# A hybrid decoder layer on one core: the last four down pairs take two token ranges behind one another, and a range's norm follows its last pair

## The chip, the cores and the metric

One core of a Trainium2 chip runs one program. TensorE (PE) multiplies into PSUM, VectorE (DVE), ScalarE (ACT) and GpSimd (POOL) work on SBUF, SyncE (SP) and GpSimd issue the DMAs here. The metric is the time of one execution on the device, in microseconds; less is better.

## The reference

One decoder layer on 16 learned meta tokens, 1024 prompt tokens and 8 x 8 sample tokens, in float32: two gated recurrent branches, their merge, then an MLP, each with an RMS norm before and after. The change is in the last part:

```python
    hn = rms_norm(x, gains[2])
    ff = jnp.square(jax.nn.relu(hn @ w_up)) @ w_down
    x = x + rms_norm(ff, gains[3])
```

`hn` is (tokens, 1024), `w_up` 1024 x 4096, `w_down` 4096 x 1024. Only the prompt tokens and the sample tokens (1088) go through the MLP.

## The kernel before, in words

Activations lie with the features on the 128 partitions and the tokens along the free axis. The tokens are cut into two halves of 544 columns, which one Strassen step treats as the two column blocks of a product; so a weight *pair* (2 x 2 blocks of 512 x 128) needs seven products instead of eight. They are taken in the order S3, S1, A11, S2, A22, S4, A12, each for the 544 columns of a half in ranges. Each operand is split into a high and a low float16 part, and a product is 4 k blocks x 3 matmuls (high x high, high x low, low x high): 12 matmuls, 84 for a pair and a range.

The MLP's hidden features are worked in four groups (`g`); each group has four up pairs, which write the squared ReLU and its Strassen sums, split, into `aoh` and `aol` (second index the operand of the product, third the up pair), and four down pairs (`o` = 0 to 3), which add into `facc`. Up to the last up pair (group 3, pair 3) columns go in two windows of 272. The split of an up window's result is finished in three parts (`rest`), during the next window; the last window's parts follow behind the loop. Its lines L1547, L1551 and L1556 (ScalarE, high parts), L1554, L1557 and L1558 (VectorE, low parts) write columns 272 to 543 of k block 3.

The last four down pairs are taken by the loop at the end. `LCH` cuts 544 columns into ranges of 272, 144 and 128. `pairc` does a pair on a range: two copies from PSUM by ScalarE (L1426, L1430), two steps by VectorE (L1428, L1432), and seven adds into `facc` (`dn_fin`, L1469 to L1475). Then the squares of the result are added up in `sacc`, and the result is scaled by the gain (ScalarE). When all four pairs of a range are done, `norm_out` normalizes it: L1659 sums over the partitions on TensorE, L424 takes the power on GpSimd, L429 broadcasts on TensorE, L1669 multiplies, L1670 adds the residual (`xr`), and L1671 stores. `norm_out` is a generator; `bgN.step`, called after each product, advances it by estimated time, so that its matmuls lie between later products.

The weights of a pair are prepared by `prep`: two of its four blocks come by DMA into `ws`, two are summed by accumulating DMAs into `sa`; ScalarE (L190) and VectorE (L191) split each operand into `sh` and `sl`; then further accumulating DMAs (GpSimd, L222, L225, L231, and SP, L228) turn the same buffers into the next operands. Both buffers are double. Pair 0's weights are split in the loop before; those of pairs 1 to 3 are all issued ahead of the last loop, into 21 slots.

TensorE's order is that of the code (`manual_schedule`). In the last loop the order of the other engines is made by a scheduler from estimated times; on the chip each engine then goes through its list.

Of the kernel before, what the change touches and what calls it, by code (L numbers as in the profile page):

```python
# [7 lines left out]
F32 = mybir.dt.float32  # L8
F16 = mybir.dt.float16
U8 = mybir.dt.uint8  # L10
AF = mybir.ActivationFunctionType
OP = mybir.AluOpType
# [3 lines left out]
P = 128  # L16
# [12 lines left out]
CQ = HW // 2  # L29
UW = 3 + NPR + NB * (3 + LS)  # L30
CW = UW - 3
NG = 4
# [6 lines left out]
LCH = [(0, 272), (272, 144), (416, 128)]  # L39
# [28 lines left out]
def layer_kernel(ctx, tc, xT, w_pl, w_pr, w_o, w_up, w_dn, gw, par, sconv, slru, shg,  # L68
                 cident, cmask, crow, yT, o_conv, o_h, o_sp, o_ss):
    nc = tc.nc  # L70
    ACT, DVE, POOL, PE = nc.scalar, nc.vector, nc.gpsimd, nc.tensor

    def sbuf(c, name, bufs=1, side="left", fine=True):
        return c.enter_context(tc.tile_pool(name=name, bufs=bufs, side=side, reuse_waits="tile" if fine else "pool"))
# [13 lines left out]
    def nm(s):  # L88
        cnt[0] += 1
        return f"{s}_{cnt[0]}"  # L90
# [156 lines left out]
    def take(**kw):  # L247
        drain(cur["gen"])
        ops = cur["ops"]
        begin(**kw)  # L250
        return ops
# [31 lines left out]
    def prod(o, op, B, nk, c0, w, first):  # L283
        h, l = op
        bh, bl = B
        for k in range(nk):
            PE.matmul(o, h[:, k, :], bh[:, k, c0:c0 + w], start=first and k == 0, stop=False,  # L287
                      skip_group_check=not first)
            PE.matmul(o, h[:, k, :], bl[:, k, c0:c0 + w], start=False, stop=False, skip_group_check=not first)  # L289
            PE.matmul(o, l[:, k, :], bh[:, k, c0:c0 + w], start=False, stop=(k == nk - 1),  # L290
                      skip_group_check=not first)
# [128 lines left out]
    def rs_pow(ps, n, pool, bias):  # L420
        t = pool.tile([P, n], F32, tag="st", name=nm("st"))
        DVE.tensor_scalar(t, ps[:, :n], bias, None, op0=OP.add)
        rs = pool.tile([P, n], F32, tag="rs", name=nm("rs"))
        POOL.tensor_tensor(rs, t, mhalf[:, :n], op=OP.pow)  # L424
        return rs

    def rs_bcast(rs, items, ps):
        for i, skip, n, off in items:
            PE.matmul(ps[:, off:off + n], rs[:, i:i + 1].to_broadcast([P, P]), ident[:, skip:skip + n],  # L429
                      start=True, stop=True)  # L430

    def chunk_tiles(w):
        starts, items = [], []
        o = 0
        while o < w:
            n = min(P, w - o)
            s = o if n == P else w - P
            items.append((len(starts), P - n, n, o))
            starts.append(s)
            o += n  # L440
        return starts, items
# [138 lines left out]
    g0, hl, hp, hk, nhk, n4sp, p2sp, rbh, ibh, gnp, g1, g2, g3 = (sm[:, i, :] for i in range(13))  # L580
# [332 lines left out]
    with tc.manual_schedule(engines={E.PE, E.DVE, E.Pool, E.Activation}):  # L913
# [28 lines left out]
        for n in range(4):  # L942
            e, c0 = n % 2, n // 2 * CT
# [321 lines left out]
    def qbank():  # L1265
        return pq.tile([P, 512], F32, tag="q", name=nm("q"))

    ep = sbuf(ctx, "ep")
# [44 lines left out]
    bgN = Steps()  # L1313
# [70 lines left out]
    for n, (c0, w) in enumerate(WIN):  # L1384
        bgN.drain(n - 2)
        for half in range(2):
            t0 = half * HW + c0
            xx = n3.tile([P, KT, WM], F32, tag=f"x2{half}", name=nm("x2c"))
            acc = n3.tile([P, 2, WM], F32, tag="acc", name=nm("acc"))
# [25 lines left out]
    def pairc(ops, B, c0, w, fin, hook=None):  # L1415
        b4, b3, b1, b2 = qbank(), qbank(), qbank(), qbank()
        U = uvp.tile([P, 2, CT], F32, tag="U", name=nm("U"))
        u, v = U[:, 0, :w], U[:, 1, :w]

        def p(b, name, bi, first):  # L1420
            prod(b[:, :w], ops[name], B(bi), 4, c0, w, first)
            if hook:
                hook(12 * (w / 2400 + 0.0025))

        p(b3, "S3", 5, True)
        ACT.activation(v, b3[:, :w], AF.Copy)  # L1426
        p(b4, "S1", 3, True)
        DVE.tensor_tensor(v, v, b4[:, :w], op=OP.add)  # L1428
        p(b1, "A11", 0, True)
        ACT.activation(u, b1[:, :w], AF.Copy)  # L1430
        p(b2, "S2", 4, True)
        DVE.tensor_tensor(u, b2[:, :w], u, op=OP.subtract)  # L1432
        p(b3, "A22", 6, False)
        p(b4, "S4", 2, False)
        p(b1, "A12", 1, False)
        fin(b1[:, :w], b3[:, :w], b4[:, :w], u, v, c0, w)
# [23 lines left out]
    def dn_fin(g, o):  # L1460
        def fin(b1, b3, b4, u, v, c0, w):
            f11, f21, f12, f22 = (mlp["facc"][:, q // 2, 2 * o + q % 2, c0:c0 + w] for q in range(4))
            if g == 0:
                DVE.tensor_tensor(f22, u, v, op=OP.subtract)
                DVE.tensor_tensor(f21, u, b3, op=OP.subtract)
                DVE.tensor_tensor(f12, b4, u, op=OP.subtract)
                ACT.activation(f11, b1, AF.Copy)
            else:
                DVE.tensor_tensor(f22, f22, u, op=OP.add)  # L1469
                DVE.tensor_tensor(f21, f21, u, op=OP.add)  # L1470
                DVE.tensor_tensor(f12, f12, u, op=OP.subtract)
                DVE.tensor_tensor(f22, f22, v, op=OP.subtract)
                DVE.tensor_tensor(f21, f21, b3, op=OP.subtract)
                DVE.tensor_tensor(f12, f12, b4, op=OP.add)
                DVE.tensor_tensor(f11, f11, b1, op=OP.add)  # L1475
        return fin
# [24 lines left out]
    facc = fp.tile([P, 2, KT, HW], F32, name="facc")  # L1501
# [128 lines left out]
    l2 = sbuf(ctx, "l2", 2)  # L1630
    lslot = (single(l1) for _ in range(21))
    lops = [take(slot=lslot)]
# [7 lines left out]
    def norm_out(c0, w, sacc):  # L1640
        starts, items = chunk_tiles(w)
        ns = len(starts)
        n = 4 if w <= 144 else 2
        todo = [(half, j) for half in (1, 0) for j in range(0, KT, n)]
        xrs = {}

        def load(i):
            if i < len(todo):
                half, j = todo[i]
                t = l2.tile([P, 576], F32, tag="xr", bufs=4, name=nm("xr"))[:, :n * w].rearrange("p (j t) -> p j t", j=n)  # L1650
                nc.sync.dma_start(t, x2_d[:, j:j + n, half * HW + c0:half * HW + c0 + w])
                xrs[i] = t

        for i in range(4):
            load(i)
        ps = qbank()
        for half in (1, 0):
            for i, s in enumerate(starts):
                PE.matmul(ps[:, half * ns + i:half * ns + i + 1], sacc[:, half, 0, s:s + P], ones, start=True, stop=True)  # L1659
        rs = rs_pow(ps, 2 * ns, l2, D * EPS * KD * KD)  # L1660
        yield 4.5
        pss = {}
        for half in (1, 0):
            pss[half] = qbank()
            rs_bcast(rs[:, half * ns:(half + 1) * ns], items, pss[half])
        for i, (half, j) in enumerate(todo):
            t0 = half * HW + c0
            f = facc[:, half, j:j + n, c0:c0 + w]
            DVE.tensor_tensor(f, f, pss[half][:, None, :w].to_broadcast([P, n, w]), op=OP.mult)  # L1669
            (POOL if i % 2 == 0 else DVE).tensor_tensor(f, f, xrs[i], op=OP.add)  # L1670
            nc.sync.dma_start(yT[:, j:j + n, t0:t0 + w], f)  # L1671
            load(i + 4)
            yield 1.5

    for c0, w in LCH:
        sacc = l2.tile([P, 2, 2, CQ], F32, tag="sacc", bufs=1, name=nm("sacc"))
        for o in range(4):
            pairc(lops[o], BA, c0, w, dn_fin(NG - 1, o), bgN.step)
            for half in (1, 0):
                src = facc[:, half, 2 * o:2 * o + 2, c0:c0 + w]  # L1680
                acc = sacc[:, half, :, :w]
                if o == 0:
                    ACT.activation(acc, src, AF.Square)
                else:
                    s = l2.tile([P, 2, CQ], F32, tag="s", name=nm("s"))
                    ACT.activation(s[:, :, :w], src, AF.Square)
                    (POOL if c0 == 0 and o < 3 else DVE).tensor_tensor(acc, acc, s[:, :, :w], op=OP.add)
                    if o == 3:
                        DVE.tensor_tensor(acc[:, 0], acc[:, 0], acc[:, 1], op=OP.add)
                for r in range(2):  # L1690
                    ACT.activation(src[:, r], src[:, r], AF.Copy, scale=g3[:, 2 * o + r:2 * o + r + 1])
        bgN.drain()
        bgN.add(norm_out(c0, w, sacc), 3.0)
    bgN.drain()


# [83 lines left out]
```

## Time and profile before

| | us |
|---|---|
| median of 3 runs | 1927.18 |
| lowest, highest | 1926.94, 1930.95 |
| the profiled execution | 1927.69 |
| its span, first to last instruction | 1925.9 |
| first matmul of the last four down pairs | about 1813.8 |

Times in rows are microseconds from the start of the span. In a row of instructions the second number is how long the group lasted; consecutive instructions of an engine overlap a little, so the step from one to the next is shorter than the duration of one. In brackets stands the idle time of the engine ahead of the row, and what ended it.

### The profile page before, as it was taken

What the parts mean: (1) busy time and instruction counts of PE and PEld (TensorE: products, weight loads), DVE (VectorE), ACT (ScalarE), POOL (GpSimd) and SP (SyncE); (2) the same over time, 40 slices, a digit from 0 to 9 for tenths busy, and PEclk for the clock granted to TensorE, in tenths of its full rate; (3) what the DMA queues carried; (4) which work ended last, traced back from release to release, by engine and by line L of the source; (5) the groups of instructions that cost most, each with busy time, mean ns of one, the idle gap of its engine ahead of it and who ended that gap; (6) DMA issues with size and microseconds to landing.
All of it is one profiled execution on the core that took longest, in us unless ns stands there. A gap on an engine that the chain in (4) does not pass through costs nothing. (4 is left out here: it accounts for less than half of the span.)

```text
span 1925.9 us, 43547 instructions
## 1 busy us (share of the span) xinstructions
PE 1780.8 (92%) x17856; PEld 1519.6 (79%) x17856; DVE 1472.3 (76%) x2654; ACT 1013.9 (53%) x2126; POOL 558.4 (29%) x626
## 2 busy tenths in 40 slices
PE   5999999999999988886899899889999999999897
PEld 4888898898888766665677689878888888888676
DVE  7998989788865888877886867697557757756767
ACT  4555555555445767754443445467346436526653
POOL 3522111211222233436442335562111111111122
PEclk9899999999999998998999999899999999999998
DMA  5252332433346433446778744234545554544635
GB/s 179 61 115 75 85 103 69 123 76 86 94 130 159 103 90 86 106 136 191 224 213 243 235 108 115 59 75 105 116 105 106 114 110 94 115 107 104 133 72 164
DMA packets 117335, 230.30 MB, mean 120 GB/s; under 512 B 11152, under 2 KB 45328, under 8 KB 114064
## 3 DMA queue, kind: packets, MB, share of 16 engines
q0 software_dynamic: 45184, 97.28, 25.6%
q1 hardware_dynamic: 62704, 125.24, 19.9%
q10 hardware_dynamic: 9248, 5.02, 1.0%
q8 instruction: 139, 2.28, 0.5%
q14 instruction: 60, 0.49, 0.1%
HBM read 191.43 MB, written 36.06 MB: 118 GB/s over the span
## 5 line engine op out<-in xcount | busy, mean ns | idle before, releaser
L289 PEld LDWEIGHTS <-sh 128*128 128x128 f16 x3920 | 387.3, 99 | 157.5 <-issue 87.1
L287 PEld LDWEIGHTS <-sh 128*128 128x128 f16 x3920 | 388.3, 99 | 82.9 <-ACT sh L190 7.0
L290 PEld LDWEIGHTS <-sl 128*128 128x128 f16 x3920 | 387.8, 99 | 80.4 <-DVE sl L191 7.6
L287 PE MATMUL pd<-tsh,sh 128*128 128x276 f16 (+1 forms) x960 | 272.4, 284 | 22.3 <-ACT th L405 8.5
L289 PE MATMUL pd<-tsl,sh 128*128 128x276 f16 (+1 forms) x960 | 272.4, 284 | 0.0
L290 PE MATMUL pd<-tsh,sl 128*128 128x276 f16 (+1 forms) x960 | 272.0, 284 | 0.0
L287 PE MATMUL q<-aoh,sh 128*128 128x272 f16 (+2 forms) x1008 | 260.5, 268 | 7.5 <-ACT sh L190 6.1
L290 PE MATMUL q<-aoh,sl 128*128 128x272 f16 (+2 forms) x1008 | 260.6, 268 | 3.6 <-DVE sl L191 3.6
L287 PE MATMUL q<-hoh,sh 128*128 128x272 f16 (+2 forms) x952 | 255.5, 273 | 6.1 <-DVE U L1518 3.6
L289 PE MATMUL q<-aol,sh 128*128 128x272 f16 (+2 forms) x1008 | 260.6, 268 | 0.0
L191 DVE SCALAR_TENSOR_TENSOR sl<-ws,sh 128x512 f16<-128x512 f32 x288 | 210.2, 733 | 63.3 <-ACT sh L190 62.6
L290 PE MATMUL q<-hoh,sl 128*128 128x272 f16 (+2 forms) x952 | 255.5, 273 | 1.0 <-DVE sl L191 1.0
L289 PE MATMUL q<-hol,sh 128*128 128x272 f16 (+2 forms) x952 | 255.5, 273 | 0.6 <-DVE hol L1288 0.6
L287 PE MATMUL pd<-xh,sh 128*128 128x276 f16 (+1 forms) x776 | 222.3, 287 | 36.2 <-ACT U L308 19.5
L191 DVE SCALAR_TENSOR_TENSOR sl<-sa,sh 128x512 f16<-128x512 f32 x201 | 151.1, 754 | 133.0 <-ACT sh L190 131.8
L289 PE MATMUL pd<-xl,sh 128*128 128x276 f16 (+1 forms) x776 | 222.7, 287 | 0.0
L190 ACT ACTIVATE sh<-ws 128x512 f16<-128x512 f32 x288 | 173.8, 622 | 92.5 <-PE pd L289 63.3
L290 PE MATMUL pd<-xh,sl 128*128 128x276 f16 (+1 forms) x776 | 222.5, 287 | 0.0
L190 ACT ACTIVATE sh<-sa 128x512 f16<-128x512 f32 x201 | 124.7, 623 | 124.3 <-DMA sa<-in_w_pr 57.1
L852 PE MATMUL pd<-sh,xh 128*128 128x128 f16 (+1 forms) x576 | 103.4, 222 | 2.3 <-ACT F L366 2.0
L854 PE MATMUL pd<-sh,xl 128*128 128x128 f16 (+1 forms) x576 | 103.5, 222 | 0.0
L853 PE MATMUL pd<-sl,xh 128*128 128x128 f16 (+1 forms) x576 | 103.4, 222 | 0.0
(360 smaller groups left out, 4243.6 us busy)
## 6 DMA issues: line engine op xcount, KB each, us to landing
sa<-in_w_pr POOLq DMA_DIRECT2D x105, 256.0 KB, 4.7
ws<-in_w_pr SPq DMA_DIRECT2D x35, 512.0 KB, 3.5
sa<-in_w_up POOLq DMA_DIRECT2D x48, 256.0 KB, 3.7
sa<-in_w_dn POOLq DMA_DIRECT2D x48, 256.0 KB, 3.8
sa<-in_w_pr SPq DMA_DIRECT2D x35, 256.0 KB, 3.3
ws<-in_w_pr POOLq DMA_DIRECT2D x35, 256.0 KB, 5.9
ws<-in_w_pr SPq DMA_DIRECT2D x35, 256.0 KB, 4.8
th<-th POOLq DMA_DIRECT2D x16, 544.0 KB, 7.1
```

The source lines that it names most:

```text
L190: ACT.activation(hi, src, AF.Copy, scale=SW)
L191: DVE.scalar_tensor_tensor(lo, src, SW, hi, op0=OP.mult, op1=OP.subtract)
L287: PE.matmul(o, h[:, k, :], bh[:, k, c0:c0 + w], start=first and k == 0, stop=False, skip_group_check=not first)
L289: PE.matmul(o, h[:, k, :], bl[:, k, c0:c0 + w], start=False, stop=False, skip_group_check=not first)
L290: PE.matmul(o, l[:, k, :], bh[:, k, c0:c0 + w], start=False, stop=(k == nk - 1), skip_group_check=not first)
L852: PE.matmul(po, a, wh[:, k % 4, :], start=(k == 0), stop=False)
L853: PE.matmul(po, a, wl[:, k % 4, :], start=False, stop=False)
L854: PE.matmul(po, b, wh[:, k % 4, :], start=False, stop=(k == KT - 1))
```

## The change

Before, a range went through all four pairs, then the next range. Now the twelve pieces are taken in this order, (pair, range): (0, 0), (0, 1), (1, 0), (1, 1), (2, 0), (3, 0), (2, 1), (3, 1), then (0, 2), (1, 2), (2, 2), (3, 2). The norm of a range is added behind its pair 3. Since two ranges are open at once, the sums of squares have two tiles, those of `EB0` and `EB1`, which the up windows used. The four adds of range 0 that GpSimd did go to VectorE.

```diff
-    for c0, w in LCH:
-        sacc = l2.tile([P, 2, 2, CQ], F32, tag="sacc", bufs=1, name=nm("sacc"))
-        for o in range(4):
-            pairc(lops[o], BA, c0, w, dn_fin(NG - 1, o), bgN.step)
...
-                    (POOL if c0 == 0 and o < 3 else DVE).tensor_tensor(acc, acc, s[:, :, :w], op=OP.add)
...
-        bgN.drain()
-        bgN.add(norm_out(c0, w, sacc), 3.0)
+    saccs = {}
+    seq = [(0, 0), (0, 1), (1, 0), (1, 1), (2, 0), (3, 0), (2, 1), (3, 1)] + [(o, 2) for o in range(4)]
+    for o, n in seq:
+        c0, w = LCH[n]
+        if o == 0:
+            sacc = ep.tile([P, 4, CQ], F32, tag=f"EB{n % 2}", name=nm("sacc"))
+            saccs[n] = sacc.rearrange("p (h r) w -> p h r w", h=2)
+        sacc = saccs[n]
+        pairc(lops[o], BA, c0, w, dn_fin(NG - 1, o), bgN.step)
...
+                DVE.tensor_tensor(acc, acc, s[:, :, :w], op=OP.add)
...
+        if o == 3:
+            bgN.drain()
+            bgN.add(norm_out(c0, w, sacc), 3.0)
     bgN.drain()
```

The lines of the last loop get other numbers: the squares L1683 and L1686 become L1690 and L1693, the adds L1687 and L1689 become L1694 and L1696, the scaling L1691 becomes L1698.

TensorE's list behind the last matmul of (0, 0), in the changed kernel: the end of the first product (S3, weights `sh_2908` and `sl_2909`) of (0, 1), third and fourth k block, with the semaphores that each row waits for.

```order
L287 LDWEIGHTS sh_2908_24711
L287 MATMUL q_2970_25015<-aoh_17418,sh_2908_24711 128x144
L289 LDWEIGHTS sh_2908_24711
L289 MATMUL q_2970_25015<-aol_17419,sh_2908_24711 128x144
L290 LDWEIGHTS sl_2909_24712
L290 MATMUL q_2970_25015<-aoh_17418,sl_2909_24712 128x144
L287 LDWEIGHTS sh_2908_24711
L287 MATMUL q_2970_25015<-aoh_17418,sh_2908_24711 128x144 [waits Activation_49]
L289 LDWEIGHTS sh_2908_24711
L289 MATMUL q_2970_25015<-aol_17419,sh_2908_24711 128x144 [waits DVE_49]
```

Before, the first product of (1, 0) stood there; now the fourth k block of (0, 1) stands there, which reads the last up window's halves and waits for ScalarE (its high part) and for VectorE (its low part).

ScalarE's list around the last window's last part (L1556), before. `sh_2934` to `sh_2938` are pair 2's S1, A11 and A22, `q_2969` and `q_2970` are PSUM tiles of (1, 0).

```order
L1683 ACTIVATE sacc_2962_24906<-facc_18240 128x544
L190 ACTIVATE sh_2934_24842<-sa_2917_24802 128x512
L190 ACTIVATE sh_2936_24847<-ws_2912_24733 128x512
L190 ACTIVATE sh_2938_24852<-ws_2912_24733 128x512
L1691 ACTIVATE facc_18240<-facc_18240,sm_117 128x272 x2
L1556 ACTIVATE aoh_17418<-ET_2916_24783 128x2x272
L1426 ACTIVATE U_2972_25017<-q_2969_25014 128x272
```

And now, up to pair 2's S2, S3 and A12 (`sh_2940` to `sh_2944`); `U_2973` belongs to (0, 1):

```order
L190 ACTIVATE sh_2934_24842<-sa_2917_24802 128x512
L190 ACTIVATE sh_2936_24847<-ws_2912_24733 128x512
L190 ACTIVATE sh_2938_24852<-ws_2912_24733 128x512
L1556 ACTIVATE aoh_17418<-ET_2916_24783 128x2x272
L1690 ACTIVATE sacc_2962_24906<-facc_18240 128x544 x2
L1698 ACTIVATE facc_18240<-facc_18240,sm_117 128x272 x4
L1426 ACTIVATE U_2973_25018<-q_2970_25015 128x144
L190 ACTIVATE sh_2940_24857<-sa_2917_24802 128x512
L190 ACTIVATE sh_2942_24862<-ws_2912_24733 128x512
L190 ACTIVATE sh_2944_24866<-ws_2912_24733 128x512
L1430 ACTIVATE U_2973_25018<-q_2971_25016 128x144
```

L1556 keeps its place behind the three splits; the copy L1430 of (0, 1) now has three more splits ahead of it.

VectorE's list between the norm of range 0 and the sums of range 1, now; `U_3034` belongs to (0, 2), `sacc_2968` holds the sums of range 1.

```order
L1670 TENSOR_TENSOR facc_18240<-facc_18240,xr_3024_25776 128x2x272
L1432 TENSOR_TENSOR U_3034_25848<-q_3033_25847,U_3034_25848 128x128
L1472 TENSOR_TENSOR facc_18240<-facc_18240,U_3020_25695 128x144
L1473 TENSOR_TENSOR facc_18240<-facc_18240,q_3017_25692 128x144
L1474 TENSOR_TENSOR facc_18240<-facc_18240,q_3016_25691 128x144
L1469 TENSOR_TENSOR facc_18240<-facc_18240,U_3034_25848 128x128
...
L1473 TENSOR_TENSOR facc_18240<-facc_18240,q_3031_25845 128x128
L1694 TENSOR_TENSOR sacc_2968_25013<-sacc_2968_25013,s_3026_25814 128x2x144
L1694 TENSOR_TENSOR sacc_2968_25013<-sacc_2968_25013,s_3027_25820 128x2x144
L1670 TENSOR_TENSOR facc_18240<-facc_18240,xr_3028_25829 128x2x272
L1696 TENSOR_TENSOR sacc_2968_25013<-sacc_2968_25013 128x144 x2
```

Before, pairs 2 and 3 of range 1 stood between that norm's last L1670 and the sums of range 1; now the sums come right behind it.

## Rows read from the trace of the kernel before

**Rows 1.** The page, part 1: busy time of each engine.
```profile
PE 1780.8 (92%) x17856; PEld 1519.6 (79%) x17856; DVE 1472.3 (76%) x2654; ACT 1013.9 (53%) x2126; POOL 558.4 (29%) x626
```

**Rows 2.** Stretches: length, busy (count) by engine, PEclk, DMA share, GB/s.
```profile
1813.84:1823.58 9.74, 9.51 (x82) 7.94 (x82) 5.46 (x12) 4.50 (x10) 1.72 (x2) 1.00 0.97 250
1823.58:1829.22 5.64, 0.57 (x5) 0.12 (x3) 4.17 (x11) 3.76 (x6) 1.72 (x2) 0.84 0.44 93
1829.22:1834.43 5.21, 5.21 (x24) 3.52 (x25) 5.21 (x10) 3.56 (x7) 0.57 (x1) 0.52 0.75 171
1852.10:1855.25 3.15, 0.69 (x5) 0.12 (x3) 1.75 (x4) 1.15 (x2) 0.86 (x1) 0.91 0.44 75
1855.25:1858.26 3.01, 3.01 (x15) 2.03 (x15) 1.24 (x3) 2.60 (x6) 1.72 (x2) 0.53 0.33 59
1870.44:1874.94 4.50, 4.50 (x75) 4.50 (x74) 1.57 (x7) 2.28 (x7) 1.36 (x1) 1.00 0.01 4
1901.05:1911.77 10.72, 10.72 (x195) 10.70 (x193) 9.58 (x28) 4.67 (x16) 2.79 (x2) 1.00 0.70 194
1911.60:1925.90 14.30, 1.71 (x14) 1.19 (x11) 6.79 (x17) 1.89 (x6) 3.20 (x3) 0.66 0.30 89
```

**Rows 3.** Waits from 1800 us on: us in total, times, longest.
```profile
ACT sh L190 <- DMA sa<-in_w_dn: 13.6, 6, 5.3
...
PE q L287 <- ACT sh L190: 6.1, 3, 3.3
```

**Rows 4.** Timeline of PE: norm matmuls, and the last matmul of the pairs.
```profile
1869.13 1.44 PE L1659 MATMUL q<-ones,sacc 128*128 128x1 f32 x12
...
1874.94 1.46 PE L429 MATMUL q<-ident,rs 128*128 128x128 f32 x12
...
1911.71 0.22 PE L290 MATMUL q<-aoh,sl 128*128 128x128 f16 x1
```

**Rows 5.** Timeline of ACT: splits of pairs 1 to 3, and L1556.
```profile
1814.08 1.14 ACT L190 ACTIVATE sh<-ws 128x512 f16<-128x512 f32 x2
...
1832.05 0.63 ACT L190 ACTIVATE sh<-sa 128x512 f16<-128x512 f32 x1 [1.09 <-DMA sa<-in_w_dn]
1832.59 1.13 ACT L190 ACTIVATE sh<-ws 128x512 f16<-128x512 f32 x2
...
1834.45 0.64 ACT L1556 ACTIVATE aoh<-ET 128x544 f16<-128x544 f32 x1
...
1839.90 0.63 ACT L190 ACTIVATE sh<-sa 128x512 f16<-128x512 f32 x1 [2.87 <-DMA sa<-in_w_dn]
1841.17 1.15 ACT L190 ACTIVATE sh<-ws 128x512 f16<-128x512 f32 x2 [0.65 <-DMA ws<-in_w_dn]
...
1851.40 0.63 ACT L190 ACTIVATE sh<-sa 128x512 f16<-128x512 f32 x1 [2.65 <-DMA sa<-in_w_dn]
...
1857.70 0.61 ACT L190 ACTIVATE sh<-sa 128x512 f16<-128x512 f32 x1
```

**Rows 6.** Timeline of DVE: the end of the last up window.
```profile
1830.03 0.43 DVE L1553 TENSOR_TENSOR ET<-ET,EB 128x272 f32<-128x272 f32 x1
...
1831.30 0.43 DVE L1475 TENSOR_TENSOR facc<-facc,q 128x272 f32<-128x272 f32 x1
...
1835.12 0.73 DVE L1558 TENSOR_TENSOR aol<-ET,aoh 128x544 f16<-128x544 f32 x1 [0.35 <-ACT aoh L1556]
```

**Rows 7.** Timeline of DVE: norm of range 0, and later sums.
```profile
1875.76 5.14 DVE L1669 TENSOR_TENSOR facc<-facc,q 128x544 f32<-128x544 f32 x8 [1.00 <-PE q L429]
...
1884.74 0.29 DVE L1432 TENSOR_TENSOR U<-q,U 128x144 f32<-128x144 f32 x1
...
1892.49 0.46 DVE L1687 TENSOR_TENSOR sacc<-sacc,s 128x288 f32<-128x288 f32 x1 [0.30 <-ACT s L1686]
...
1893.46 0.52 DVE L1689 TENSOR_TENSOR sacc<-sacc 128x144 f32<-128x144 f32 x2
1894.37 0.29 DVE L1432 TENSOR_TENSOR U<-q,U 128x128 f32<-128x128 f32 x1 [0.39 <-ACT U L1430]
```

More of the change, by code (lines that the diff above doesn't have):

```diff
@@ L1673, in norm_out @@
             yield 1.5
-    for c0, w in LCH:
-        sacc = l2.tile([P, 2, 2, CQ], F32, tag="sacc", bufs=1, name=nm("sacc"))
-        for o in range(4):
-            pairc(lops[o], BA, c0, w, dn_fin(NG - 1, o), bgN.step)
[L1679 to L1686, printed above, removed]
-                    (POOL if c0 == 0 and o < 3 else DVE).tensor_tensor(acc, acc, s[:, :, :w], op=OP.add)
[L1688 to L1691, printed above, removed]
-        bgN.drain()
-        bgN.add(norm_out(c0, w, sacc), 3.0)
+    saccs = {}
[7 more added lines that the diff above has]
+        pairc(lops[o], BA, c0, w, dn_fin(NG - 1, o), bgN.step)
+        for half in (1, 0):
+            src = facc[:, half, 2 * o:2 * o + 2, c0:c0 + w]
+            acc = sacc[:, half, :, :w]
+            if o == 0:
+                ACT.activation(acc, src, AF.Square)
+            else:
+                s = l2.tile([P, 2, CQ], F32, tag="s", name=nm("s"))
+                ACT.activation(s[:, :, :w], src, AF.Square)
+                DVE.tensor_tensor(acc, acc, s[:, :, :w], op=OP.add)
+                if o == 3:
+                    DVE.tensor_tensor(acc[:, 0], acc[:, 0], acc[:, 1], op=OP.add)
+            for r in range(2):
+                ACT.activation(src[:, r], src[:, r], AF.Copy, scale=g3[:, 2 * o + r:2 * o + r + 1])
+        if o == 3:
+            bgN.drain()
+            bgN.add(norm_out(c0, w, sacc), 3.0)
     bgN.drain()
```

## Prediction

> **What bounds the kernel now.** I read the busy shares first. TensorE is busy for 92% of the span and VectorE for 76% [rows 1], so the change can only act where TensorE stands still. It touches nothing before the last four down pairs, so I went on to their stretch, 1813.8 us to the end. I write (o, n) for down pair o on token range n; range 0 is 272 columns wide, range 1 144, range 2 128. The table by stages shows four things. (0, 0) ran at full clock, 84 matmuls in 9.74 us. Then TensorE did almost nothing from 1823.58 to 1829.22. When it came back its granted clock was 0.52 for 5.21 us, the 1.2 GHz level, and then 1.00. From 1852.10 to 1855.25 it stood again, and 0.53 followed for 3.01 us [rows 2]. The waits name the cause: TensorE waited for ScalarE's weight splits (L190), and ScalarE for the weight DMAs, 13.6 us in six waits [rows 3]. The prep of one pair's weights is a chain of splits and accumulating DMAs, and it sets the pace here.
>
> How much is there to win? The work left behind (0, 0), at full clock: three pairs of 9.74 us; four of range 1 at 84 x 0.0625 = 5.25 us (six products of 12 matmuls fill the 4.50 us stretch of [rows 2]); four of range 2 at 84 x 0.056 = 4.7 us (16 products of 12 fill the 10.72 us stretch); and the norms' small matmuls of ranges 0 and 1, 1.3 + 1.3 us [rows 4] and by their width about 0.87 + 0.87. Sum: 29.2 + 21.0 + 18.8 + 4.3 = 73.3 us. It took from 1823.58 to the last matmul's start at 1911.71 [rows 4], 88.1 us. So waits and low clock cost 14.8 us, and behind the last matmul 14.3 us of norm and stores [rows 2] follow that the change doesn't touch.
>
> **The change, step by step.** The idea that the rows suggest is good: (0, 1) needs only weights that are there, and 5.25 us of it would cover the wait at 1823.58. But a pair needs data too, and each engine's order is in front.md. I go along TensorE.
>
> *(0, 1) meets a gate.* Its first product takes, as fourth k block, the split halves of up pair 3 for columns 272 to 543, the last up window. They are written by ScalarE L1556 and VectorE L1558. In the trace these ran at 1834.45 and 1835.12 [rows 5, 6]; before, nobody needed them until range 1 at 1866. In the new order L1556 stands behind the same three splits, which begin when the DMA lands at 1832.05 and end at 1833.6 (1832.59 and two issue steps of 0.52). So L1556 runs at 1833.6 to 1834.3, and L1558, behind the third split's low half, at 1834.8 to 1835.5. TensorE gets through 9 of 84 matmuls (to 1824.1) and then stands until 1835.5, but for one matmul: **11.3 us**. The DMAs ahead of this point and their issues are the same in both orders, so their landing is taken as it was.
>
> Could TensorE do other work meanwhile? The rows say no: at 1827 it sat waiting for the first product of (1, 0), although the weights of that pair's third and fifth products had been split at 1814.08 [rows 3, 5]. The Trainium skill, TensorE: Matmul & The Clock Gate, in the section on the array (engine queue depths), says that TensorE reorders weight loads only, that matmuls keep their order, and that ScalarE and VectorE are strictly first in, first out. The trace agrees (L1553, which feeds L1556, ended at 1830.46, and L1556 ran at 1834.45); if engines could reach past a waiting instruction, the gate would be nearly free and the time 1927, which is rival C.
>
> *The clock behind it.* After 5.1 us of standing, 24 matmuls at the low level took 5.21 us, against 2.78 at the other: 2.4 us lost. Lower bound for a stand of 11.3 us: the same. Upper bound: no row shows one so long in this stage, so I allow twice that. I take **2.6 us**.
>
> *The rest of (0, 1) and (1, 0).* ScalarE's copy L1430 and VectorE's L1428 of (0, 1) now stand behind the split of pair 2's S2, whose DMA lands at 1839.90, and L1430 also behind two more at 1841.17 [rows 5]. TensorE, at the low clock, comes to the products that need them at 1841.2 and 1842.0: 0.7 and 0.4 us. L1430 of (1, 0) stands behind pair 3's S2 (1851.40 [rows 5]) and is needed at 1851.6: 0.4 us. Together **1.5 us**. (0, 1) ends near 1843.3 and (1, 0) near 1853.7; the weights of pair 1 cost no wait any more.
>
> *(1, 1) meets the next queue.* Its fifth product needs L1426, which stands behind pair 3's last split (1857.0 by its DMA, 1857.70 as it ran [rows 5]) and behind two squares of (1, 0). These wait for L1474 and L1475, which stand behind that split's low half on VectorE. From 1857.0: 0.6 split, 0.7 low half, 0.35 L1474, two squares of 0.55, and the copy, so 1860.2. TensorE arrives at 1853.7 + 48 x 0.0625 = 1856.7 and stands **3.5 us**; after the 2.5 us stand of the trace 3.01 us at the low clock lost 1.5, so **1.5** again. Then (2, 0) and (3, 0) run through, since all weights are there.
>
> *The norm of range 0.* Before, it had 18 products of range 1 ahead of it after its broadcast (L429) until range 2 began. Now L429 stands in (3, 1), four products before range 2. The sums of range 1 (L1696) stand behind all of that norm on VectorE, and TensorE's L1659 for range 1 stands in (0, 2). VectorE needs: from the first L1669 to the end of the third L1670 as in the trace, 1875.76 to 1884.74, 9.0 us, contention included [rows 7]; then L1432, three steps of range 1 at 0.22, five of range 2 at 0.20, two adds at 0.4, one L1670 at 0.64 and 0.5 for the last two sums: 3.8 us [rows 7]. With 0.8 us from L429 to L1669 that is 13.6 us behind L429's start. TensorE has 1.3 (L429) + 48 x 0.0625 + 60 x 0.056 = 7.7 us of work there: it stands **5.9 us**. Bounds: 5 if VectorE and GpSimd don't disturb each other, 7 if each step does. The clock behind it: **2.6 us**, as above.
>
> *What costs nothing.* Four adds move from GpSimd to VectorE (0.64 us each). They stand in (1, 1), (2, 0) and after, where VectorE has room: 5.46 us of work in the 9.74 us of a pair [rows 2]; without that cover they cost 2.6 us. The sums of squares now lie in the tiles EB0 and EB1; EB0 is free when VectorE has read it for the last time, just ahead of L1475 (1831.30 [rows 6]), and the first square comes at 1834. No DMA is issued earlier or later by the code; stores move with the norm.
>
> **Sum.** 11.3 + 2.6 + 1.5 + 3.5 + 1.5 + 5.9 + 2.6 = 28.9 us in place of 14.8, so 14.1 us longer. The profiled execution took 1927.69 us (span 1925.9 and 1.8 around it), 0.5 above the median of 1927.18: 1941.8 against it, **1941 us** against the median.
>
> **Rivals.** *A, the gate alone:* the waits up to (1, 1) come as said, but range 1's sums are in time, because VectorE gets ahead while TensorE stands, or its stand is hidden in (0, 2). Takes off 5.9 + 2.6: 1932.8 us. For it speaks that VectorE is idle in parts; against it, that its backlog begins only with L429. 12%. *B, the clock stays low for longer:* if the low level held from 1835.5 through (1, 0), 74 x 0.0625 + 84 x 0.11 = 13.9 us in place of 2.6, 1952 us. Against it speak two stands after which the clock came back within 5.21 us. 6%. *C, engines reach past the gate, or the gate opens early:* 1941 - 11.3 - 2.6 = 1927, no change. Against it stand the rows above. 5%. *D, faster:* the DMA that frees the three splits lands 8 us earlier than at 1832.05, so that L1556 is done before (0, 1) needs it. Then the weight waits are covered and only the norm's 5.9 + 2.6 us stay of 28.9, with 1.5 of small ones: 1927.2 - 14.8 + 10.0 = 1922 us. It decides from a landing before 1824. Nothing ahead of that DMA changes; 4%.
>
> **Chances.** The forecast as it stands, 1935 to 1948, 73%. The range for 8 in 10 reaches to A below: 1932 to 1948, which leaves out C, D, half of A's spread and most of B. About 0.2% (3.9 us) is what a measurement of this kernel can tell from no change: faster 0.05, within it 0.06, slower 0.89.
>
> **What would show it.** In the profile after: TensorE waiting some 10 us for ScalarE L1556 and 1 us for VectorE L1558 near 1835; about 5 us at clock 0.5 after it; a wait for L1426 near 1860; a wait of 5 to 7 us for L1696 before L1659 in range 2; the three waits for L190 of pairs 1 to 3 gone; the last matmul near 1926, and 14 us behind it as before. I am wrong if (0, 1) starts without a stand, if the DMA chain itself gets shorter, or if the low clock costs far more than 2.6 us a time.

## The result, and the profile after

The changed kernel takes 1941.07 us (median of 6, 1937.45 to 1948.96), the kernel before, on the same chip, 1927.06 us (median of 6, 1922.82 to 1931.72). The ratio is 1.0074, with a 95% interval of 1.0052 to 1.0097: slower by 10 to 19 us, 14 in the middle. The forecast was 1941 us.

The profiled execution of after is the quickest of its six, 1937.45 us (span 1935.7), 9.76 above the one of before. The work ahead of the last four down pairs is the same code, but it reached this stage 3.1 us earlier. So I compare from the end of (0, 0) on. To the start of the last matmul it took 100.4 us (1820.46 to 1920.88), against 88.1 before [rows 4]; from there to the end of the span 14.8 against 14.2 [rows 2, 4]. The stage itself is thus 12.3 us longer and its tail 0.6; less the 3.1 us these are the 9.8, and the medians' 14.0 lie 1.1 above the 12.9, inside the scatter of single runs.

The page of after, part 1, to be set beside [rows 1]: no engine has more to do, but for the four adds that went from GpSimd to VectorE.

```profile
PE 1776.8 (92%) x17856; PEld 1520.8 (79%) x17856; DVE 1473.2 (76%) x2658; ACT 1014.2 (52%) x2126; POOL 556.5 (29%) x622
```

The stretches of after, columns as in [rows 2]: (0, 0); the stand behind it; what followed; (1, 1) with its stand; what followed; the stand at the norm; what followed; the tail.

```profile
1810.72:1820.46 9.74, 9.51 (x82) 8.04 (x83) 5.46 (x12) 5.06 (x12) 1.72 (x2) 1.00 0.97 260
1820.46:1831.15 10.69, 1.19 (x14) 0.89 (x12) 10.35 (x21) 8.00 (x16) 3.46 (x4) 0.67 0.61 141
1831.15:1834.60 3.45, 3.45 (x33) 3.45 (x32) 0.32 (x1) 1.69 (x5) 0.86 (x1) 0.53 1.07 219
1847.91:1855.40 7.49, 3.37 (x52) 3.22 (x51) 5.58 (x13) 3.35 (x7) 0.15 (x1) 0.96 0.23 39
1855.40:1858.40 3.00, 3.00 (x28) 3.00 (x27) 2.00 (x8) 1.62 (x5) 0.00 (x0) 0.52 0.00 0
1894.80:1903.59 8.79, 2.11 (x15) 1.94 (x12) 7.06 (x20) 2.00 (x6) 2.50 (x2) 0.75 1.03 322
1903.59:1906.17 2.58, 2.58 (x27) 2.58 (x26) 0.45 (x2) 0.91 (x3) 1.02 (x1) 0.52 0.99 306
1920.88:1935.70 14.82, 2.38 (x12) 1.82 (x9) 6.63 (x16) 1.89 (x6) 3.20 (x3) 0.58 0.30 89
```

There are three stands where before had two, and behind each the granted clock is 0.52 or 0.53, the 1.2 GHz level, for some 3 us. The waits of TensorE in after from 1800 us on (total, times, longest) name them:

```profile
PE q L1659 <- DVE sacc L1696: 8.6, 2, 6.7
PE q L287 <- ACT aoh L1556: 8.2, 1, 8.2
PE q L287 <- ACT U L1426: 4.1, 1, 4.1
PE q L289 <- DVE aol L1558: 1.3, 1, 1.3
...
PE q L287 <- ACT U L1430: 0.9, 1, 0.9
```

The waits for L190 of [rows 3] are gone. In their place stand the gate (L1556, L1558), the copies (L1426, L1430) and the sums of range 1 (L1696; 6.7 us of the 8.6, the rest is the tail's). ScalarE's timeline of after shows what stood ahead of the first two, as [rows 5] did for before:

```profile
1819.89 0.63 ACT L190 ACTIVATE sh<-sa 128x512 f16<-128x512 f32 x1 [3.96 <-DMA sa<-in_w_dn]
1820.43 0.64 ACT L1540 ACTIVATE EB<-EB 128x544 f32<-128x544 f32 x1
...
1827.08 0.63 ACT L190 ACTIVATE sh<-sa 128x512 f16<-128x512 f32 x1 [1.21 <-DMA sa<-in_w_dn]
1827.62 1.13 ACT L190 ACTIVATE sh<-ws 128x512 f16<-128x512 f32 x2
1828.66 0.64 ACT L1556 ACTIVATE aoh<-ET 128x544 f16<-128x544 f32 x1
...
1850.86 0.63 ACT L190 ACTIVATE sh<-sa 128x512 f16<-128x512 f32 x1 [0.92 <-DMA sa<-in_w_dn]
1853.83 1.20 ACT L1693 ACTIVATE s<-facc 128x544 f32<-128x544 f32 x2 [2.34 <-DVE facc L1474]
1854.93 0.27 ACT L1426 ACTIVATE U<-q 128x144 f32<-128x144 f32 x1
```

L1556 runs behind pair 2's three splits, which begin when the DMA lands at 1827.08. Even the start of the window's finish (L1540) had stood behind a split of pair 1 that waited 3.96 us. L1426 of (1, 1) runs behind pair 3's last split and two squares, which wait for VectorE's L1474. VectorE's timeline of after shows L1558 (beside [rows 6]), L1474 behind that split's low half (L191), and the norm (beside [rows 7]):

```profile
1830.19 0.71 DVE L1558 TENSOR_TENSOR aol<-ET,aoh 128x544 f16<-128x544 f32 x1
...
1852.76 0.68 DVE L191 SCALAR_TENSOR_TENSOR sl<-sa,sh 128x512 f16<-128x512 f32 x1
1853.36 0.43 DVE L1474 TENSOR_TENSOR facc<-facc,q 128x272 f32<-128x272 f32 x1
...
1888.03 5.13 DVE L1669 TENSOR_TENSOR facc<-facc,q 128x544 f32<-128x544 f32 x8 [1.00 <-PE q L429]
...
1898.97 1.81 DVE L1694 TENSOR_TENSOR sacc<-sacc,s 128x288 f32<-128x288 f32 x2
1900.71 0.71 DVE L1670 TENSOR_TENSOR facc<-facc,xr 128x544 f32<-128x544 f32 x1
1901.35 0.51 DVE L1696 TENSOR_TENSOR sacc<-sacc 128x144 f32<-128x144 f32 x2
```

From the first L1669 VectorE had no idle time until the second L1696 ended at 1901.86. TensorE had reached L1659 at 1894.9; it ran from 1901.69, when the first L1696 was done.

### The profile page after: what moved, and what is told of

It is laid out like the page before. It is cut to its first block, busy times and chain, and to the rows that moved or that the text cites. A ratio compares the mean times of both kernels' runs of the same rounds, so it can differ in the third digit from the quotient of the medians.

```text
span 1935.7 us, 43542 instructions
## 1 busy us (share of the span) xinstructions
PE 1776.8 (92%) x17856; PEld 1520.8 (79%) x17856; DVE 1473.2 (76%) x2658; ACT 1014.2 (52%) x2126; POOL 556.5 (29%) x622
## 5 line engine op out<-in xcount | busy, mean ns | idle before, releaser
L191 DVE SCALAR_TENSOR_TENSOR sl<-ws,sh 128x512 f16<-128x512 f32 x288 | 209.0, 729 | 67.4 <-ACT sh L190 67.0
L191 DVE SCALAR_TENSOR_TENSOR sl<-sa,sh 128x512 f16<-128x512 f32 x201 | 152.9, 762 | 132.9 <-ACT sh L190 129.5
L190 ACT ACTIVATE sh<-ws 128x512 f16<-128x512 f32 x288 | 173.7, 621 | 92.7 <-PE pd L289 60.9
L190 ACT ACTIVATE sh<-sa 128x512 f16<-128x512 f32 x201 | 124.7, 623 | 126.9 <-DMA sa<-in_w_pr 66.2
```

The source lines that it names most:

```text
L190: ACT.activation(hi, src, AF.Copy, scale=SW)
L191: DVE.scalar_tensor_tensor(lo, src, SW, hi, op0=OP.mult, op1=OP.subtract)
```

## The experiments

Theory T: the loss is three queue waits which the order of pieces makes (the gate at (0, 1), L1426 at (1, 1), L1696 ahead of L1659), with the low clock behind each. Rivals: the small edits cost (R1), interleaving costs wherever the gate is (R2), the gate is all (R3), VectorE is the bound at the end (R4), and, after the first four runs, the chain of splits and DMAs is the bound and only moves its wait (R5), or an earlier finish of the last window helps in any order (R6). Below, the *stage* is the time from the end of (0, 0) to the start of the last matmul, the *tail* what follows to the end of the span, each in the profiled execution. The first four expectations are written in us against a before of 1927.1; the chips of the experiments gave 1922.6 to 1924.1, so ratios are compared.

| kernel | ratio to before | 95% interval | stage | tail |
|---|---|---|---|---|
| before | 1 | | 88.1 | 14.2 |
| after | 1.0074 | 1.0052 to 1.0097 | 100.4 | 14.8 |
| e1_adds_tiles | 1.0004 | 0.9992 to 1.0017 | 86.5 | 14.5 |
| e2_gate_order | 1.0023 | 1.0006 to 1.0039 | 92.2 | 14.5 |
| e3_rest_first | 1.0052 | 1.0035 to 1.0068 | 95.3 | 14.4 |
| e4_norm_late | 1.0062 | 1.0043 to 1.0081 | 96.6 | 15.4 |
| e5_rest_and_queue | 1.0038 | 1.0021 to 1.0054 | 92.8 | 14.4 |
| e6_best | 1.0015 | 1.0001 to 1.0029 | 86.7 | 16.4 |
| e7_before_rest | 1.0006 | 0.9993 to 1.0019 | 88.0 | 14.2 |
| e8_queue_only | 1.0056 | 1.0037 to 1.0074 | 99.1 | 14.4 |
| e9_best2 | 1.0013 | 1.0000 to 1.0027 | 85.2 | 16.0 |
| e10_rest_chain | 1.0056 | 1.0040 to 1.0071 | 93.6 | 14.6 |
| e11_chain_kept | 0.9983 | 0.9967 to 0.9998 | 81.5 | 16.1 |

The same stage of before took 86.5 to 88.1 us in before, e1 and e7, which have its order of pieces: differences of a microsecond or two between stages are not read as effects.

**e1_adds_tiles**: before, with the small edits alone.

```diff
-        sacc = l2.tile([P, 2, 2, CQ], F32, tag="sacc", bufs=1, name=nm("sacc"))
+        sacc = ep.tile([P, 4, CQ], F32, tag=f"EB{nsac[0] % 2}", ...
-                    (POOL if c0 == 0 and o < 3 else DVE).tensor_tensor(acc, acc, s[:, :, :w], op=OP.add)
+                    DVE.tensor_tensor(acc, acc, s[:, :, :w], op=OP.add)
```

> The order of pieces of before, with only the small edits of the change: the two tiles EB0 and EB1 for the sums, and the four adds on VectorE. Theory T (the change costs three waits that its order of pieces makes: the gate L1556/L1558 at (0,1), L1426 at (1,1), L1696 ahead of L1659): none of them can arise, so 1927 us, ratio 0.999 to 1.001. Rival R1 (the moved adds or the tiles carry part of the 14 us): four adds of 0.64 us in full, 2.6 us, 1929.7 (1.0013) or more, with a longer prep chain since the adds stand between the low halves of the splits.

Measured: 1.0004, that is 0.8 us more, from -1.5 to +3.3. None of the three waits occurs. R1's 2.6 us can't be excluded by the time alone, but they are at most a quarter of the 14; the stage shows nothing of them.

**e2_gate_order**: after, with (1, 0) ahead of (0, 1).

```diff
-    seq = [(0, 0), (0, 1), (1, 0), (1, 1), ...
+    seq = [(0, 0), (1, 0), (0, 1), (1, 1), ...
```

> After, with (1,0) taken ahead of (0,1). T: the gate is no longer met (9.5 us and about 1.5 at low clock go), and the weight wait of before is back in front of (1,0) (5.1 to 5.6 us and 2.4 at low clock); the norm's 6.7 and 1.3 stay; L1426 at (1,1) (4.1 and 1.4) may stay or go. So 1941.1 - 11.0 + 7.8 = 1938 us if it stays, 1932 if it goes. Rival R2 (interleaving two ranges costs by itself, wherever the gate is): 1941, and the rows for L1556 would be replaced by others of the same size. Rival R3 (the gate is all): 1927 to 1930.

Measured: 1.0023; against after's 1.0074 that is about 10 us less, at the lower of T's two values. The waits of TensorE in e2 from 1800 us on:

```profile
PE q L1659 <- DVE sacc L1696: 9.0, 2, 7.1
PE q L287 <- ACT sh L190: 2.2, 1, 2.2
PE q L287 <- ACT U L1430: 1.7, 1, 1.7
```

The gate is not in the list: L1556 ran at 1831.80, and (0, 1) asked for it at 1840. The weight wait is back, and the norm's wait is as it was. This one exchange of two pieces shows that the gate belongs to the place of (0, 1): R2 falls. R3 falls too, since the 7.1 us at the norm remain.

**e3_rest_first**: after's order of pieces, but the last window's finish is put ahead of pair 1's second split and all later ones in the lists of ScalarE and VectorE (`issue_after` places what follows behind the given instruction in the list of its engine).

```diff
-                ACT.activation(hh[:, 5:7], t[1], AF.Copy)
+                last["ra"] = ACT.activation(hh[:, 5:7], t[1], AF.Copy)
...
     lops = [take(slot=lslot)]
-    for o in range(1, 4):
-        if o < 3:
-            lops.append(take(slot=lslot))
+    advance(cur["gen"], 3)
+    with tc.issue_after(last["ra"].ins), tc.issue_after(last["rv"].ins):
+        for o in range(1, 4):
+            if o < 3:
+                lops.append(take(slot=lslot))
```

> After, with the order of pieces kept, but the last up window's rest (L1540 to L1558) put ahead of pair 1's second split and all later ones in the lists of ScalarE and VectorE. T: the gate falls away (9.5 and 1.5 us), (0,1) runs at once and covers the weight wait; the queue wait at (1,1) may change by 3 us either way, the norm's 6.7 and 1.3 us stay: 1924 to 1932 us. Rival R2 (it isn't the place in the queue; the rest itself comes late, or the delayed splits cost as much): 1938 to 1942.

Measured: 1.0052, a miss of the size: some 4 us won, not 9 or more. The waits of TensorE in e3:

```profile
PE q L1661 <- DVE sacc L1698: 8.4, 2, 6.5
PE q L287 <- ACT U L1426: 5.6, 2, 4.0
PE q L289 <- DVE aol L1558: 1.9, 1, 1.9
PE q L287 <- DVE U L1428: 1.2, 1, 1.2
```

The gate did open: 1.9 us in place of 9.5. But (1, 0) and (1, 1) now came earlier to copies that stood behind splits, as ScalarE's timeline shows: L1426 of (1, 1) behind pair 2's last and pair 3's first three splits, which began when a DMA landed at 1844.00.

```profile
1844.00 1.15 ACT L190 ACTIVATE sh<-sa 128x512 f16<-128x512 f32 x2 [1.19 <-DMA sa<-in_w_dn]
1845.06 1.13 ACT L190 ACTIVATE sh<-ws 128x512 f16<-128x512 f32 x2
1846.71 0.66 ACT L1695 ACTIVATE s<-facc 128x544 f32<-128x544 f32 x1 [0.51 <-DVE facc L1474]
1847.27 0.27 ACT L1426 ACTIVATE U<-q 128x144 f32<-128x144 f32 x1
```

So T named the gate rightly and took its gain for additive, which it isn't: this engine's list has the next DMA wait a few microseconds on. The waits for copies came to 6.8 us (L1426 and L1428), in after to 5.0 (L1426 and L1430), and the low clock behind them and behind the norm cost 2.6 and 2.3 us, in after 1.4 and 1.2.

**e4_norm_late**: after, with the norm of range 1 begun behind (0, 2).

```diff
         if o == 3:
-            bgN.drain()
-            bgN.add(norm_out(c0, w, sacc), 3.0)
+            if n != 1:
+                bgN.drain()
+            if n == 1:
+                late1 = (c0, w, sacc)
+            else:
+                bgN.add(norm_out(c0, w, sacc), 3.0)
+        if (o, n) == (0, 2):
+            bgN.drain()
+            bgN.add(norm_out(*late1), 3.0)
```

> After, with the norm of range 1 begun only behind (0,2), so that L1659 for it stands in (1,2), 60 to 84 matmuls of 0.056 us later. T: its wait of 6.7 us falls to 2 or less and the low clock behind it (1.3) goes with it: 5 to 8 us less, 1933 to 1936 us. Rival R4 (VectorE is the bound there, and the wait only moves to a later L1659 or to the copies of range 2): 1939 to 1941.

Measured: 1.0062, whose interval contains after's value; by the traces the stage is 3.8 us shorter and the tail 0.6 longer. The wait for L1696 fell from 6.7 to 2.4 us, and the one in the tail rose from 1.9 to 3.0. T has the mechanism, and R4 has a part: about a quarter of the 4.3 us came back in the tail. The rest of the shortfall lies ahead of the norm, where the edit changes nothing: L1426 took 4.7 us in place of 4.1, and the low clock behind the gate and behind L1426 cost 2.3 and 2.0 us in place of 1.6 and 1.4.

**e5_rest_and_queue**: e3, with the splits of pairs 2 and 3 behind the copies of the piece ahead (`last["c"]` is L1430 of the last piece).

```diff
-        ACT.activation(u, b1[:, :w], AF.Copy)
+        last["c"] = ACT.activation(u, b1[:, :w], AF.Copy)
...
+    def more(o, n):
+        if (o, n) in ((1, 0), (1, 1), (2, 0)):
+            with tc.issue_after(last["c"].ins):
+                if (o, n) == (1, 0):
+                    advance(cur["gen"], 3)
+                elif (o, n) == (1, 1):
+                    lops.append(take(slot=lslot))
+                    advance(cur["gen"], 3)
+                else:
+                    drain(cur["gen"])
+                    lops.append(cur["ops"])
...
         pairc(lops[o], BA, c0, w, dn_fin(NG - 1, o), bgN.step)
+        more(o, n)
```

> e3_rest_first, and the splits of pairs 2 and 3 come in the lists behind the copies of the piece ahead: pair 2's first three behind L1430 of (1,0), its others and pair 3's first three behind L1430 of (1,1), pair 3's last four behind L1430 of (2,0). T: the waits of e3 for L1426 (5.6 us in two) and L1428 (1.2), and some 2.8 us of low clock behind them, go, since no split that waits for a DMA stands ahead of a copy that TensorE needs; 1 to 3 us for the weights of (2,0) or (3,0) may come back, since the chain of splits and DMAs stays as long; the norm's 6.5 us stay. So 7 to 9 us less than e3: ratio to before 1.000 to 1.002. Rival R5 (the chain of DMAs is the bound, and moves its wait to wherever the weights are needed): as e3, 1.004 to 1.006.

Measured: 1.0038, between T and R5. L1426 costs 1.9 us in place of 5.6, but TensorE now waits 2.3 us for ScalarE and 1.1 for VectorE at the weights of (3, 0) and (2, 0): holding the splits back made the chain late (pair 3's S3 was split 37.3 us behind the end of (0, 0), at 1857.78, in e3 32.3 behind it).

**e6_best**: e5, with the adds of (0, 0) behind L1558, and the norm of range 1 as in e4 but at 5.5 in place of 3.0.

```diff
+    def behind_rest(fin):
+        def f(*a):
+            with tc.issue_after(last["rv"].ins):
+                fin(*a)
+        return f
...
-        pairc(lops[o], BA, c0, w, dn_fin(NG - 1, o), bgN.step)
+        fin = dn_fin(NG - 1, o)
+        if (o, n) == (0, 0):
+            fin = behind_rest(fin)
+        pairc(lops[o], BA, c0, w, fin, bgN.step)
...
-            bgN.add(norm_out(*late1), 3.0)
+            bgN.add(norm_out(*late1), 5.5)
```

> e5_rest_and_queue, with the seven adds of (0,0) behind the rest's last step L1558 on VectorE, and the norm of range 1 as in e4_norm_late but 2.5 us later still. T: L1558's 1.9 us fall to 0.5, the norm's 6.5 and 2 us of low clock fall to 2 or less, the tail behind the last matmul grows by 1 to 2 us: 5 to 7 us less than e5, ratio to before 0.996 to 0.999, faster than both. Rival R4 (VectorE is the bound at the end): as e5, 1.000 to 1.002.

Measured: 1.0015, no gain over before. Against e5 it is some 4 us, a little under the expectation: the stage is 6.1 shorter, the tail 2.0 longer. The wait for L1558 is gone, but three for L1428 (3.6 us) came, and the wait of (1, 0) for L1426 was 2.9 us there.

**e7_before_rest**: the edit of e3 in the order of pieces of before.

> Before, with the last window's rest ahead of pair 1's second split and the later ones, as in e3 but in the order of pieces of before. T: nothing needs columns 272 to 543 until range 1, so no gain; pair 1's weights, which (1,0) waits for, come up to 2 us later: ratio 1.000 to 1.002. Rival R6 (what e3 won is a gain of the earlier rest in any order): 0.997.

Measured: 1.0006, as T said. The early finish is worth nothing by itself; R6 falls.

**e8_queue_only**: after, with `more` of e5 and without the edit of e3.

> After, with the splits of pairs 2 and 3 behind the copies as in e5, but with the rest left where it was among pair 1's splits. T: the three splits of pair 2 no longer stand ahead of L1556, only pair 1's last one does (1825.24 in the trace of after, 4.8 us behind the end of (0,0)); so the stand at (0,1) falls from 9.5 to about 6 us, the waits for L1430 (0.9) and L1426 (4.1 and 1.4 of low clock) go: 9 to 11 us less than after, ratio to before 1.002 to 1.003; with 1 to 3 us of new weight waits up to 1.004. Rival R5: 1.006 or more.

Measured: 1.0056, a miss of the size again. The waits of TensorE in e8:

```profile
PE q L1666 <- DVE sacc L1704: 8.5, 2, 6.6
PE q L287 <- ACT aoh L1556: 5.3, 1, 5.3
PE q L287 <- ACT sh L190: 2.6, 1, 2.6
PE q L289 <- DVE aol L1558: 2.2, 1, 2.2
```

The waits for L1430 and L1426 are gone, as T said, and the gate is 7.5 in place of 9.5. But 2.6 us for pair 3's weights come back, as R5 said (its S3 was split 43.1 us behind the end of (0, 0), in after 28.3), and the low clock behind the gate lasted 43 matmuls (5.1 us, 2.4 lost) in place of 28.

**e9_best2** and **e10_rest_chain** ask whether the chain was late because of GpSimd's queue, where L180 of the next pair had come ahead of L231. e10 is e3 with this edit, e9 is e6 with it and with pair 1's last split behind the copies of (1, 0).

```diff
+        last3 = st["unit"] >= len(units) - 3
...
-            sum_load()
+            if not last3:
+                sum_load()
...
-            nc.gpsimd.dma_start(q, src[:, 3], accum_op=OP.add)
+            d = nc.gpsimd.dma_start(q, src[:, 3], accum_op=OP.add)
+            if last3:
+                with tc.issue_after(d.ins):
+                    sum_load()
```

> e6_best, with two edits to the weight chain: GpSimd issues the second accumulating DMA of a pair (L231) ahead of the next pair's first load (L180) instead of behind it, and pair 1's last split stands behind the copies of (1,0), which use it last. If the chain of splits and DMAs was 5 us late in e3, e5 and e6 because of that place in GpSimd's queue (pair 1's last split 10.6 us behind its second in e5, 5.3 in after), then the wait for L1426 at (1,0) (2.9 us, 1.5 behind it), most of that for the low half at (2,0) (1.1) and of that at (3,0) (2.9) go: 5 to 8 us less than e6, ratio to before 0.997 to 0.999. Rival R5 (the chain is as long in any queue order): 1.000 to 1.002.

> e3_rest_first, with L231 ahead of the next pair's L180 on GpSimd. If the shortfall of e3 (4 us won where 9 to 11 were expected) came from the chain that its edit made 5 us later, its waits for L1426 and L1428 (6.8 us and 2.8 of low clock) fall by 3 to 7 us: ratio to before 1.001 to 1.004. If they come from the place of the copies behind splits alone, as in after: 1.004 to 1.006.

Measured: e10 1.0056, in the range of its second case. The start of the chain did get shorter (pair 1's last split ran 6.7 us behind its second, in e3 10.4), but the waits for L1426 came to 6.8 us, now 0.9 and 5.9, where in e3 those for L1426 and L1428 had come to that. ScalarE's timeline of e10, whose L1431 is L1426 of after, L1435 its L1430 and L1700 its L1693:

```profile
1837.88 0.63 ACT L190 ACTIVATE sh<-sa 128x512 f16<-128x512 f32 x1 [1.96 <-DMA sa<-in_w_dn]
1841.14 0.63 ACT L190 ACTIVATE sh<-sa 128x512 f16<-128x512 f32 x1 [2.63 <-DMA sa<-in_w_dn]
1841.67 1.13 ACT L190 ACTIVATE sh<-ws 128x512 f16<-128x512 f32 x2
1842.71 0.64 ACT L1700 ACTIVATE s<-facc 128x544 f32<-128x544 f32 x1
1843.26 0.27 ACT L1431 ACTIVATE U<-q 128x144 f32<-128x144 f32 x1
```

The copy, for which TensorE had waited from 1837.6, ran behind pair 3's splits, which had waited for a landing at 1841.14. The copy needs nothing of these splits. But e10 alone doesn't separate its two cases: further on the chain was no shorter than in e3. Pair 3's first split ran 24.7 us behind the end of (0, 0), in e3 23.2, and its S3 32.4, in e3 32.3. That the place of the copies makes the wait is shown by e11 below, where the same split ran 24.4 us behind that end. e9 (1.0013, R5's case) has the reverse fault: its copies are free, but pair 2's second split, held behind L1430 of (1, 1), ran 20.1 us behind the end of (0, 0) where in e10 it ran 16.3 behind it, pair 3's S3 35.2 in place of 32.4, and TensorE waited 3.3 us for it.

**e11_chain_kept**: e10 with the norm of e6, and with each split held back only as far as a copy needs it; `last["c1"]` is L1426 of the last piece, `last["c"]` its L1430.

```diff
+        if (o, n) == (1, 0):
+            with tc.issue_after(last["c1"].ins):
+                advance(cur["gen"], 6)
+        elif (o, n) == (1, 1):
+            with tc.issue_after(last["c1"].ins):
+                lops.append(take(slot=lslot))
+            with tc.issue_after(last["c"].ins):
+                advance(cur["gen"], 3)
+        elif (o, n) == (2, 0):
+            with tc.issue_after(last["c"].ins):
+                drain(cur["gen"])
+                lops.append(cur["ops"])
```

> e10_rest_chain (rest first, L231 ahead of L180), with the norm of range 1 as in e6_best, and with the splits held back only where a copy that TensorE needs would stand behind one that waits for its DMA: pair 2's behind L1426 of (1,0), pair 3's first three behind L1430 of (1,1), its others behind L1430 of (2,0). By the landings of e10 (pair 2's first split 1827.2, pair 3's 1841.1, 46.5 and 48.9 for its later ones, its (0,0) ending at 1816.4) none of them is delayed, so the chain stays as it is there, while e5, e6 and e9 held it back by some 8 us. If both things bound the stage, the copies' place and the chain: the waits of e10 for L1426 (6.8 us and 2 of low clock) go to 1 to 2, one of about 1 us for pair 3's S3 at (3,0) comes, and the norm gives back 4: 10 us less than e10, 3 to 5 less than before, ratio 0.997 to 0.999. Rival R5 (the chain moves its wait to wherever the weights are needed, whatever the place of the copies): 1.001 to 1.003.

The 8 us said there of e5, e6 and e9 were misread, from times that were not counted from the end of (0, 0): at pair 3's S3 the chain was 2.8 us late in e9 and 5 in e5. Measured: 0.9983, interval 0.9967 to 0.9998, as expected: faster than both kernels, by 3.3 us against before (0.4 to 6.3). The upper end lies close to 1; the stage, 81.5 us against 86.5 to 88.1 in the three kernels with the order of before, bears it out. The waits of TensorE in e11 (L1675 is the norm's L1659, L1433 the L1428 of after, L1563 its L1558):

```profile
PE q L1675 <- DVE sacc L1713: 3.5, 1, 3.5
PE q L292 <- DVE U L1433: 2.5, 2, 1.5
PE q L294 <- DVE aol L1563: 1.9, 1, 1.9
PE q L292 <- ACT U L1431: 1.8, 1, 1.8
...
PE q L292 <- ACT U L1435: 0.9, 1, 0.9
```

No wait for weights is left, and the largest, 3.5 us, lies in the tail. The stretches of e11, (0, 1) to (1, 1), (2, 0) to the first part of (0, 2), the rest of range 2, the tail, show the clock at 1.00 up to the last matmul:

```profile
1817.67:1842.95 25.28, 20.72 (x255) 18.82 (x253) 17.55 (x40) 16.44 (x38) 5.24 (x6) 1.00 0.54 116
1842.95:1878.86 35.91, 35.91 (x423) 32.89 (x421) 26.98 (x65) 16.19 (x40) 6.60 (x7) 1.00 0.24 54
1879.00:1899.23 20.23, 17.64 (x293) 17.24 (x291) 18.09 (x52) 9.08 (x30) 6.63 (x5) 1.00 0.69 210
1899.23:1915.30 16.07, 2.14 (x11) 1.60 (x8) 7.89 (x20) 1.89 (x6) 3.20 (x3) 0.62 0.60 169
```

Of the stage's 81.5 us (88.1 in before), 73.3 are work by the prediction's sum. The tail takes 1.9 of the 6.6 us back.

## Why the prediction was right, point by point

The sum was 28.9 us lost in the stage; after lost 100.4 - 73.3 = 27.1. The terms of the table add up to 26.3 as measured; 0.8 us is in none of them. The sum's terms, with what the trace of after measured (the low clock as the time of the slow matmuls less 0.0625 or 0.056 us for each):

| term | predicted | measured |
|---|---|---|
| the gate at (0, 1) | 11.3 | 8.2 + 1.3 = 9.5 |
| low clock behind it | 2.6 | 1.6 (28 matmuls) |
| small waits for copies | 1.5 | 0.9 |
| L1426 at (1, 1) | 3.5 | 4.1 |
| low clock behind it | 1.5 | 1.4 (25 matmuls) |
| L1659 for L1696 | 5.9 | 6.7 |
| low clock behind it | 2.6 | 1.2 (25 matmuls) and 0.9 on L1659 itself |

*The gate* was right in place and order, and 1.8 us too large. The step "their landing is taken as it was" is the one that was off: the DMA that frees the three splits landed 6.6 us behind the end of (0, 0) (1827.08), before 8.5 (1832.05 [rows 5]). From that landing to L1556 it took 1.58 us, where 1.55 had been worked out. In e1, with the order of pieces of before, the landing came 6.9 us behind the end of (0, 0), so the order of pieces did not make it earlier. Of the 1.9 us, 1.4 stand already in the load for pair 1's S2 (L222): it was issued 8.3 us ahead of that end in before, e1 and after alike, ahead of anything that the change touches, and took 9.1 us to land in before, 7.8 and 7.7 in e1 and after. The prediction had read one execution in which that load was slow; where the other 0.5 us come from is open. That TensorE did not reach past the gate is plain here: pair 1's S3 had been split at 1822.07, its low half at 1823.98, and (1, 0) with it stood unused while the gate held to 1829.35. Rival C falls with it. By the Trainium skill, TensorE: Matmul & The Clock Gate, section "Step-by-step: what each phase is for", matmuls stay in program order; the trace agrees with these 8.2 us. e2 shows the gate gone when (0, 1) comes later, e3 when its feeders come earlier.

*L1426 and the norm* were right within 0.8 us, the norm inside its bounds of 5 and 7. For L1426 that is in part luck: from the landing to the copy's end 3.2 us had been worked out, with VectorE free for the low half, and it took 4.3 (1850.86 to 1855.20), since the low half stood behind five adds until 1852.76; TensorE arrived 0.3 us behind the landing and not 0.3 ahead of it, which hid 0.6 of the difference. e4 shows that the norm's wait follows from when L1659 asks, e5 and e8 that L1426's comes from the splits ahead of it. Rival A falls with the 6.7 us. *The low clock* was right behind (1, 1) and too large behind the other two; rival B's case didn't come. *What costs nothing*: e1's 0.8 us (-1.5 to 3.3) agrees. *The tail* is 0.6 longer, which nothing of the sum held; that lies within the spread of such tails (14.2 to 14.5 with before's order of pieces, 14.4 to 14.8 with after's and its norm). Rival D had the right direction (the DMA landed earlier, by 1.9 us), and not its 8 us.

That the median met the forecast to 0.1 us is luck. The stage was 12.3 us longer, not 14.1, and single runs of after lie between 1937 and 1949. Of the signs of being wrong that the prediction named, one came in part: the DMA chain was shorter, by the 1.9 us. The stretch at the low clock behind the gate was 3.2 us and not 5.

What the prediction's sum does not show is that the terms are not independent. e3, e8 and e9 each removed a wait and won less than half of what was expected, since the next wait in ScalarE's list, or the chain's own length, came forward. The idea of the change, a piece that needs only weights that are there, is worth something once that list fits it (e11). e11's parts can be read from its neighbours. Against e10, whose chain is as long, L1426 fell from 6.8 to 1.8 us and 1.9 of low clock behind it went, while 0.9 for L1430 came: some 6 us for the free copies. In the same step the norm's 6.7 us and the low clock behind them gave way to 2.5 for L1428. Against e9, whose copies are free and whose norm is late too, the stage is 3.7 us shorter. That is the undisturbed chain, with two small edits of e9 that e11 leaves out: 4.2 us of weight waits and 2.5 of low clock behind them are gone, and the waits for L1558, L1426 and L1430 take 4.6 in their place. These are readings of waits; no run has the free copies and the undisturbed chain without the late norm.

## What to carry to other kernels

Before work is moved under a wait, list everything that it needs, its data as well as its weights, and follow each of these back through the list of its engine to the DMA that stands ahead: here a 0.6 us copy cost 8.2 us because three splits with an unfinished load came first. An in-order engine that feeds the critical one should take what is ready ahead of what waits for a load, but the load's own chain must not be held back for that; e5 and e9 did the first alone and stayed slower than the kernel before, e11 did both and was faster. A gain of several waits removed is not their sum: after each, read again which comes next.

## What the runs showed of the hardware

The stretch at the 1.2 GHz level behind a stand didn't grow with the stand. In after, stands of 9.5, 4.1 and 6.7 us were followed by 3.2, 2.9 and 2.5 us of it; in e8 one of 7.5 us by 5.1, in e2 one of 7.1 us by 4.3 and one of 3.6 us by 5.9, in before one of 5.1 us by 5.2 [rows 2]. The prediction had allowed more for a longer stand. It isn't the same in every execution either: in e4, whose code is that of after up to the norm, stands of 9.3 and 4.7 us were followed by 4.8 and 4.1 us of it. In e1 a stand of 2.2 us was followed by 3.3 us at a granted clock of 0.50, while in e7 one of 2.7 us left it at 1.00, as five stands of 0.9 to 1.9 us did in e11.

Of two accumulating loads that GpSimd issued half a microsecond apart, the second took twice as long to land as the first: in e3 L180 (issued at 1824.42) took 3.5 us and L231 (1824.96) 7.0; in e10, with the two exchanged, L231 (L233 there, 1819.93) took 3.5 and L180 (1820.47) 6.7. In after, where they were issued 1.9 us apart, they took 3.7 and 3.6. The next two of e10 (1834.35 and 1834.88), behind which SyncE issued no load for 8.8 us, took 3.5 and 6.2.
